# The second product of an MLP by Strassen's seven products, in one layer on one core

## The chip, the cores and the metric

The kernel runs on one core of a Trainium2 chip. The core has a matrix engine (TensorE, PE in the rows, with its weight loads as PEld), a vector engine (VectorE, DVE), an activation engine (ScalarE, ACT), a general engine (GpSimd, POOL) and SyncE (SP), which here only issues transfers. The metric is the device time of one execution in microseconds: 2275.08 us, the median of 3 runs (2274.39 to 2277.69).

## The reference, cut to what matters

One encoder layer in float32, with 512 tokens and a model width of 2048. Token mixing (two kinds of attention and an output projection), an MLP, and a gated injection follow each other, each between two norms. The change concerns the MLP alone:

```python
m = rms_norm(h, pre_mlp_norm[i]) @ w_up[i]            # 512 x 2048 by 2048 x 8192
m = jnp.square(jax.nn.relu(m)) @ w_down[i]            # 512 x 8192 by 8192 x 2048
h = h + rms_norm(m, post_mlp_norm[i])
```

The second line is the product in question: 512 tokens, a sum over 8192 hidden values, 2048 output columns.

## The kernel before, in words

Every product is computed to float32 accuracy from two halves: `split_out` (lines 191 to 193) writes a rounded high half `hi` on ScalarE (a copy to a type that TensorE takes) and the remainder `lo` on VectorE. A product of two such pairs is three matmuls, hi by hi, hi by lo and lo by hi (`mm3`, line 135). Weights arrive as tiles of 128 partitions by 1024 columns (512 KB), which hold two chunks of 128 rows by 512 output columns; `weights` (line 111) loads one into a buffer `raw` (3 of them) through SP's queue and splits it into two pairs `hi`, `lo` (4 buffers each).

The first product (lines 699 to 807) already runs by Strassen's seven products in Winograd's form: tokens, sum and output are cut into halves, sums of quarters are formed, and seven products take the place of eight. Its weight sums come about in two ways: an accumulating transfer that POOL issues (`accum_op`), or an addition on VectorE (lines 757 and 766). The squared hidden values go through the tensors `hdr` in HBM, which `h_out` (line 642) writes by transfers of 128 KB.

The second product (lines 810 to 852) is plain. It walks over eight blocks `fb` of eight chunks of the hidden values. For each block it loads the hidden values from `hdr` into `hring`, splits them into `hT`, and calls `tokmajor` (line 140): for each of four column pieces `n` of 512, four token tiles `i` of 128 accumulate in four PSUM banks over the block's eight chunks, then `d_done` adds them into `M` in SBUF on VectorE (line 839; a copy in the first block, line 837). The last block also takes the squares for the norm, multiplies by the gain `gpost` and starts the residual and the next norm (lines 840 to 846). The gains `gpost` and `gpre` are loaded at block 1, behind a part of `M` (`behind`, line 208, a tiny copy on POOL that makes a transfer wait).

The order of the instructions of each engine is laid out ahead of the run by a planner. It takes the program's order as the priority and a simulated time as the moment when each instruction could go, so an instruction may stand earlier or later than it is written. At run time each engine, and each transfer queue, takes its instructions in the planned order. On SBUF, tiles that carry one tag share memory: `O0`, `O1`, `X0` and `X1` are four large areas. In the first product `O0` holds the operands of products 5 and 6, `O1` those of 7 and 3, `X1` those of 1 and 2, `X0` the weight ring. A tile that takes over an area waits for the last reader of the one before. PSUM has eight banks: four with the tag `pj`, three `at`, one `o`.

## Time and profile before

| what | value |
|---|---|
| median of 3 runs | 2275.08 us |
| the profiled execution's own time | 2274.45 us |
| its span, first to last instruction | 2272.7 us |
| mean granted TensorE clock | 0.991 |
| TensorE busy | 2220.0 us (98%) |
| VectorE busy | 1375.5 us (61%) |
| ScalarE busy | 1091.3 us (48%) |
| first matmul of the second product | 1355.66 us |
| moved by transfers | 356.84 MB, 157 GB/s |

All rows below come from one profiled execution. Times within it count from its first instruction. Busy time is the time in which at least one instruction of the engine was running; matmuls overlap, so their count and their distance from each other say more than the duration of one. "Idle before" names the time an engine stood before the instructions of a group and what ended it. A granted clock of 1.00 is 2.4 GHz, 0.50 is 1.2 GHz.

### The profile page before, as it was taken

How to read it: one execution, taken by the hardware profiler on the slowest of the kernel's cores; microseconds unless marked ns; L12 is line 12 of the kernel's file. 1: busy time of each engine (PE TensorE's matmuls, PEld its weight loads, DVE VectorE, ACT ScalarE, POOL GpSimd, SP SyncE). 2: the span in 40 equal slices, each digit the busy share in tenths (PEclk: the TensorE clock that was granted, in tenths of full speed). 3: DMA queues.
4: the chain of work that ended last, by engine and by line, in shares of the span. 5: the costliest groups of instructions: out<-in, count | busy, mean ns of one | idle time of the engine just before them, and what ended most of it. 6: DMA issues, size and time to landing. Idle time of an engine off the chain costs nothing.

```text
span 2272.7 us, 30004 instructions
## 1 busy us (share of the span) xinstructions
PE 2220.0 (98%) x10899; PEld 1864.6 (82%) x10899; DVE 1375.5 (61%) x2248; ACT 1091.3 (48%) x2079; POOL 258.4 (11%) x385
## 2 busy tenths in 40 slices
PE   9999999999996799999999999999999999999997
PEld 7888888888785688888888888888888888888885
DVE  7567545555758677777777784443434434468446
ACT  5335433345656466666666673322323223257434
POOL 4320000000001121222122210000000000011002
PEclk9999999999998899999999999999999999999999
DMA  6222232236767988888887745434434433355435
GB/s 216 84 75 65 66 94 79 88 98 223 244 198 215 296 228 210 218 213 217 216 217 215 211 140 205 131 95 137 130 102 131 138 93 99 97 182 188 149 93 185
DMA packets 102084, 356.84 MB, mean 157 GB/s; under 512 B 13280, under 2 KB 14816, under 8 KB 101296
## 3 DMA queue, kind: packets, MB, share of 16 engines
q1 hardware_dynamic: 84432, 296.92, 41.1%
q0 software_dynamic: 17360, 58.01, 11.7%
q8 instruction: 85, 1.39, 0.3%
q14 instruction: 63, 0.52, 0.1%
q10 hardware_dynamic: 144, 0.01, 0.0%
HBM read 328.69 MB, written 26.18 MB: 156 GB/s over the span
## 4 chain that ended last, share of the span: by engine, by line
PE 91%; DVE 4%; ACT 1%; issue 1%; DMA 1%; POOL 1%; SPq 0%; DVEq 0%; ACTq 0%; POOLq 0%
PE tm L137 17%; PE tm L138 17%; PE tm L136 17%; PE ua L637 9%; PE ua L638 5%; PE ug L637 4%; PE ug L638 3%; PE qk L138 3%; PE qk L136 3%; PE qk L137 3%; PE ub L637 2%; PE ub L638 1%; PE ua L640 1%; DVE lo L131 1%; PE ug L640 1%
## 5 line engine op out<-in xcount | busy, mean ns | idle before, releaser
L130 ACT ACTIVATE hi<-raw 128x512 fp32r<-128x512 f32 x664 | 415.7, 631 | 806.6 <-PE tm L138 513.9
L131 DVE TENSOR_TENSOR lo<-raw,hi 128x512 fp32r<-128x512 f32 x664 | 454.1, 695 | 570.4 <-ACT hi L130 569.3
L137 PE MATMUL tm<-lo,hT 128*128 128x512 f32 x1024 | 398.6, 390 | 0.3 <-DVE lo L131 0.3
L138 PE MATMUL tm<-hi,hT 128*128 128x512 f32 x1024 | 398.3, 389 | 0.0
L136 PE MATMUL tm<-hi,hT 128*128 128x512 f32 x1024 | 370.8, 389 | 0.0
L637 PE MATMUL ua<-xc,uh 128*128 128x512 f32 x868 | 313.3, 396 | 15.8 <-ACT uh L192 15.8
L638 PE MATMUL ua<-xc,ul 128*128 128x256 f32 x992 | 259.1, 282 | 0.0
L137 PEld LDWEIGHTS tm<-lo,hT 128*128 128x128 f32 x1024 | 192.2, 188 | 40.6 <-DVE lo L131 0.7
L136 PEld LDWEIGHTS tm<-hi,hT 128*128 128x128 f32 x1024 | 192.2, 188 | 40.1 <-ACT hi L130 0.3
L138 PEld LDWEIGHTS tm<-hi,hT 128*128 128x128 f32 x1024 | 192.3, 188 | 39.8
L637 PEld LDWEIGHTS ua<-xc,uh 128*128 128x128 f32 x868 | 164.4, 189 | 49.5 <-ACT uh L192 16.6
L638 PEld LDWEIGHTS ua<-xc,ul 128*128 128x128 f32 x992 | 188.2, 190 | 13.6 <-DVE ul L193 0.9
L193 DVE TENSOR_TENSOR ul<-ring,uh 128x512 fp32r<-128x512 f32 x240 | 161.6, 689 | 55.7 <-PE ub L638 43.1
L637 PE MATMUL ug<-xc,uh 128*128 128x512 f32 x448 | 162.5, 397 | 10.4 <-ACT uh L192 10.4
L192 ACT ACTIVATE uh<-ring 128x512 fp32r<-128x512 f32 x240 | 148.6, 629 | 47.8 <-PE ub L640 25.2
L193 DVE TENSOR_TENSOR ul<-T,uh 128x512 fp32r<-128x512 f32 x192 | 130.1, 691 | 49.1 <-ACT uh L192 45.9
L192 ACT ACTIVATE uh<-T 128x512 fp32r<-128x512 f32 x192 | 117.3, 628 | 66.2 <-PE ua L637 39.3
L638 PE MATMUL ug<-xc,ul 128*128 128x256 f32 x512 | 133.9, 282 | 3.5 <-DVE ul L193 3.5
L137 PE MATMUL tm<-lo,xa 128*128 128x512 f32 x320 | 126.0, 394 | 4.5 <-DVE lo L131 4.5
L138 PE MATMUL tm<-hi,xa 128*128 128x512 f32 x320 | 125.4, 392 | 0.0
L136 PE MATMUL tm<-hi,xa 128*128 128x512 f32 x320 | 122.9, 394 | 1.0 <-ACT hi L130 0.6
L637 PEld LDWEIGHTS ug<-xc,uh 128*128 128x128 f32 x448 | 85.1, 190 | 27.1 <-ACT uh L192 10.7
(263 smaller groups left out, 3840.0 us busy)
## 6 DMA issues: line engine op xcount, KB each, us to landing
raw<-in_w_down SPq DMA_DIRECT2D x136, 512.0 KB, 3.6
ring<-in_w_up SPq DMA_DIRECT2D x128, 512.0 KB, 4.4
raw<-in_w_o SPq DMA_DIRECT2D x64, 512.0 KB, 4.0
raw<-in_w_gate SPq DMA_DIRECT2D x48, 512.0 KB, 4.2
raw<-in_w_in_t SPq DMA_DIRECT2D x39, 512.0 KB, 3.7
raw<-in_w_in_f SPq DMA_DIRECT2D x32, 512.0 KB, 3.6
hdr<-h POOLq DMA_DIRECT2D x128, 128.0 KB, 6.2
T<-in_w_up SPq DMA_DIRECT2D x32, 512.0 KB, 6.9
```

The lines of the kernel that those rows point to most:

```text
L130: nc.scalar.activation(hi, x, AF.Copy)
L131: nc.vector.tensor_sub(lo, x, hi.bitcast(F32))
L136: nc.tensor.matmul(o, lh, rh, start=start, stop=False)
L137: nc.tensor.matmul(o, lh, rl, start=False, stop=False)
L138: nc.tensor.matmul(o, ll, rh, start=False, stop=stop)
L192: nc.scalar.activation(hi, src, AF.Copy)
L193: nc.vector.tensor_sub(lo, src, hi.bitcast(F32))
L637: nc.tensor.matmul(o, hi[:, c], x, start=first and j == 0, stop=False, **on)
L638: nc.tensor.matmul(o[:, :256], lo[:, c], x[:, :256], start=False, stop=False, **on)
L640: nc.tensor.matmul(o, hi[:, c], x, start=False, stop=True, **on)
```

## The change

The second product is now computed by the same seven products. Tokens are cut into halves of 256 (`t`), output columns into halves of 1024 (`h`, each with two pieces `n` of 512), and the chunks of the sum into two halves by `half_of`: of each four chunks in a row, the first two belong to half 0 and the other two to half 1. A pair is one chunk of each half. There are 32 pairs. Blocks of 8, 8, 8 and 4 pairs go by seven products; the last four pairs (eight chunks) go through `tokmajor` as before, with the last block's `d_done`.

`hdr` is laid out by quarter, so that one transfer of 1 MB reads a quarter of a block's hidden values into `quad`. `op_work` forms the sums of quarters on VectorE and splits them into an operand `opt` (two operands share the tile `opt`). The products run in the order 1, 5, 6, 3, 7, 2, 4. The weight tiles stand in `xr` and `yr`, eight slots each: a slot's tile is loaded into `xr`, used by product 1, added to by an accumulating transfer of POOL, used by product 5, added to by VectorE (`sum_x`, after a lag of three slots), used by products 6 and 4; `yr` is loaded, added to by POOL after product 3, and loaded anew after product 7. `half_tiles` hands out buffers for the split halves of the weight tiles in turns of seven: four times a pair `hi` and `lo`, three times a `raw` buffer that holds both. A step of the loop over `todo` prepares the operand of the step two ahead (`AHEAD`), takes its share of `op_work` for the next product, and issues the twelve matmuls of its tile. Products 6, 7 and 4 accumulate onto the PSUM banks of product 1, product 3 onto those of product 5. After each product `add_out` takes each bank into `M` with a sign: on VectorE, or as a scaled copy on ScalarE for products 1, 5, 6 and 4 of the first block. The gains are loaded after the seven products.

```diff
-    hdr = [dram.tile([P, FB, S], F32, name=f"hdr{b}") for b in range(NFB)]
+    hdr = [dram.tile([P, 4, HB, 256], F32, name=f"hdr{b}") for b in range(FF // P // 2 // HB)]
+    def half_of(f):
+        return f // 2 % 2, 2 * (f // 4) + f % 2
...
-        nc.gpsimd.dma_start(hdr[f // FB][:, f % FB, t * 256:(t + 1) * 256], src)
+        odd, g = half_of(f)
+        nc.gpsimd.dma_start(hdr[g // HB][:, 2 * t + odd, g % HB, :], src)
...
     M = xo.tile([P, NT, D], F32, tag="O1", name="M")
+    NP2 = FF // P // 2
+    wdn = lambda n, odd, g: a["w_down"][n, g + odd]
+    blocks = [(g, min(HB, NP2 - CP - g)) for g in range(0, NP2 - CP, HB)]
+    ORDER = (1, 5, 6, 3, 7, 2, 4)
+    with phase("phdn") as pd:
+        quad = xo.tile([P, 4, HB, 256], F32, tag="O0", name="quad")
+        usum = pd.tile([P, HB, 256], F32, name="usum")
+        xr = xo.tile([P, 8, 1024], F32, tag="X0", name="xr")
+        yr = pd.tile([P, 8, 1024], F32, name="yr")
+        opt = xo.tile([P, 2, 2, HB, 256], F32R, tag="X1", name="opt")
...
+            n = halves[0]
+            halves[0] += 1
+            if n % 7 < 4:
+                return [wp.tile([P, 512], F32R, tag=t, name=f"d{t}{n}", bufs=NW) for t in ("hi", "lo")]
+            t = wp.tile([P, 2, 512], F32R, tag="raw", name=f"dhl{n}", bufs=NWRAW)
+            return [t[:, 0], t[:, 1]]
...
+                if p == 5:
+                    w.append(lambda Q=Q, U=U: V.tensor_sub(U, Q[A22], Q[A21]))
+                    w.append(lambda Q=Q: V.tensor_sub(Q[A21], Q[A11], Q[A21]))
+                elif p == 6:
+                    w.append(lambda Q=Q, U=U: V.scalar_tensor_tensor(Q[A11], U, -1.0, Q[A11], **minus))
+                elif p == 3:
+                    w.append(lambda Q=Q, U=U: V.scalar_tensor_tensor(U, Q[A12], -1.0, Q[A11], **minus))
+                w.append(lambda o=o, k=k, x=x: split_out(o[:, 0, k], o[:, 1, k], x))
...
+            if first and p in (1, 5, 6, 4):
+                nc.scalar.activation(m, o, AF.Copy, scale=float(sign))
+            elif sign > 0:
+                nc.vector.tensor_add(m, m, o)
+            else:
+                nc.vector.tensor_sub(m, m, o)
...
+            x = yr[:, slot] if p in (3, 7, 2) else xr[:, slot]
+            if p in (6, 4):
+                while late and (slot in late):
+                    sum_x(late.popleft())
+            w = parts2(x)
+            if p == 1:
+                nc.gpsimd.dma_start(x, wdn(n + 2, 0, g), accum_op=ALU.add)
+                nc.sync.dma_start(yr[:, slot], wdn(n + 2, 1, g))
+            elif p == 3:
+                nc.gpsimd.dma_start(x, wdn(n + 2, 0, g), accum_op=ALU.add)
+            elif p == 7:
+                nc.sync.dma_start(x, wdn(n, 1, g))
+            elif p == 4 and b + 1 < len(blocks):
+                g1, c1 = blocks[b + 1]
+                n1, kk = divmod(slot, c1 // 2)
+                if n1 < 2:
+                    x_load(n1, slot, g1 + 2 * kk)
+            if p in (5, 2):
+                late.append(slot)
+                if len(late) > LAG:
+                    sum_x(late.popleft())
...
+        for q in (A11, A22, A21, A12):
+            load_quad(0, q)
+            if q == A11:
+                for f in op_work(0, 0):
+                    f()
+                for n in range(2):
+                    for kk in range(4):
+                        x_load(n, n * 4 + kk, 2 * kk)
...
+                if b + 1 < len(blocks) and s >= 3:
+                    for q in {3: (A11,), 4: (A21,), 5: (A12,), 6: (A22,)}[s]:
+                        load_quad(b + 1, q)
+            if x + AHEAD < len(todo):
+                ready.append(operand(todo[x + AHEAD]))
+            left = c - slot
+            for _ in range(-(-len(work) // max(1, left - 2))):
+                if work:
+                    work.popleft()()
...
+            for j in range(2):
+                k = 2 * kk + j
+                hi, lo = w[j]
+                for i in range(2):
+                    t = slice(i * P, (i + 1) * P)
+                    sh, sl = op[:, 0, k, t], op[:, 1, k, t]
+                    o = acc[bank, i, n]
+                    nc.tensor.matmul(o, sh, hi, start=fresh and k == 0, stop=False, **on)
+                    nc.tensor.matmul(o, sh, lo, start=False, stop=False, **on)
+                    nc.tensor.matmul(o, sl, hi, start=False, stop=k == c - 1, **on)
...
-        GFB = 1
-        hring = xo.tile([P, 4, 2, S], F32, tag="X0", name="hring")
-        for fb in range(NFB):
...
+        gpost = bcast(pn, a["post_mlp"], D, "gpost2", M[:, 3, :])
+        gpre = bcast(pn, a["pre_ple"], D, "gpre2", M[:, 3, :])
...
+        tokmajor(lambda k, i: tuple(hT[:, q, hk[k], i * P:(i + 1) * P] for q in range(2)),
+                 wk("w_down"), ks, [(range(4), [0]), (range(4), [1]), ([0, 1], [2, 3]), ([2, 3], [2, 3])], d_done)
```

## Rows read from the trace of the kernel before

**Rows 1.** The page: busy time of three engines over the span, and TensorE and VectorE in 40 equal slices, in tenths.

```profile
PE 2220.0 (98%) x10899; PEld 1864.6 (82%) x10899; DVE 1375.5 (61%) x2248; ACT 1091.3 (48%) x2079; POOL 258.4 (11%) x385
...
PE   9999999999996799999999999999999999999997
...
DVE  7567545555758677777777784443434434468446
```

**Rows 2.** Windows of 100 us, one in the first product and two in the second: PE, PEld, DVE, ACT and POOL busy (instructions), then the granted clock, the share of the transfer engines and GB/s.

```profile
1000.00:1100.00 100.00, 100.00 (x575) 87.60 (x574) 77.57 (x120) 68.42 (x134) 21.85 (x33) 1.00 0.82 214
1400.00:1500.00 100.00, 100.00 (x443) 82.84 (x442) 41.43 (x63) 27.25 (x45) 0.00 (x0) 1.00 0.38 116
1900.00:2000.00 100.00, 100.00 (x443) 82.85 (x442) 39.50 (x59) 26.09 (x46) 0.00 (x0) 1.00 0.31 95
```

**Rows 3.** TensorE's waits in the whole run: what waited for what, us in total, times, the longest.

```profile
PE ua L637 <- ACT uh L192: 15.8, 2, 9.9
PE ug L637 <- ACT uh L192: 10.4, 1, 10.4
PE tm L137 <- DVE lo L131: 5.6, 6, 1.9
...
PE tm L136 <- ACT hi L130: 2.2, 4, 0.8
```

**Rows 4.** VectorE's timeline in the second product: start, us, instruction. The first additions into `M` of two column pieces in a row, and one in between.

```profile
1460.88 0.69 DVE L839 TENSOR_TENSOR M<-M,tm 128x512 f32<-128x512 f32 x1
1462.24 0.69 DVE L839 TENSOR_TENSOR M<-M,tm 128x512 f32<-128x512 f32 x1 [0.67 <-PE tm L138]
...
1482.64 0.69 DVE L839 TENSOR_TENSOR M<-M,tm 128x512 f32<-128x512 f32 x1
```

**Rows 5.** Timeline at the start of the first product: VectorE's 1024-wide and 512-wide operations back to back (merged, with their number at the end), and a 1024-wide copy on ScalarE.

```profile
734.18 3.50 DVE L193 TENSOR_TENSOR xc<-Af,xc 128x1024 fp32r<-128x1024 f32 x3
...
756.11 2.50 DVE L193 TENSOR_TENSOR ul<-ring,uh 128x512 fp32r<-128x512 f32 x4 [8.27 <-ACT uh L192]
...
734.31 1.06 ACT L192 ACTIVATE xc<-Af 128x1024 fp32r<-128x1024 f32 x1 [1.82 <-DVE Af L713]
```

**Rows 6.** Groups of instructions from 800 to 1300 us (first product): busy us, mean ns of one, idle time before them and what ended it.

```profile
L193 DVE TENSOR_TENSOR ul<-ring,uh 128x512 fp32r<-128x512 f32 x204 | 137.6, 689 | 40.1 <-PE ub L638 38.5 <-ACT uh L192 1.2
...
L192 ACT ACTIVATE uh<-ring 128x512 fp32r<-128x512 f32 x203 | 125.9, 629 | 38.6 <-PE ub L640 22.5 <-PE ug L637 10.2 <-PE ua L637 4.3
...
L757 DVE TENSOR_TENSOR T<-T,ring 128x1024 f32<-128x1024 f32 x26 | 31.9, 1225 | 0.9
...
L750 POOL DMA_DIRECT2D ring<-in_w_up x26 | 23.2, 891 | 248.8 <-DMA ring<-in_w_up 133.3 <-DVE h L658 68.1 <-DVE ul L193 27.1
```

**Rows 7.** Transfers. First the window of 10 us in which the transfer engines were full (columns as in rows 2), then, for 1000 to 1100 us, the two queues (packets, MB, share of 16 engines) and the issues with KB each and the median us to landing.

```profile
740.00:750.00 10.00, 4.70 (x16) 3.69 (x16) 3.75 (x4) 1.15 (x2) 0.87 (x1) 0.55 0.98 381
...
q1 hardware_dynamic: 3650, 13.26, 43.1%
q0 software_dynamic: 2434, 8.01, 38.0%
...
ring<-in_w_up POOLq DMA_DIRECT2D x6, 512.0 KB, 7.3
...
hdr<-h POOLq DMA_DIRECT2D x22, 128.0 KB, 6.6
T<-in_w_up POOLq DMA_DIRECT2D x5, 512.0 KB, 5.9
```

**Rows 8.** The handover between the two products: the copy behind the last group's product 6, SP's first transfer into the area of the weight ring, the last matmul of the first product and the first of the second.

```profile
1344.93 0.60 ACT L772 ACTIVATE kb<-ua 128x512 f32<-128x512 f32 x1 [1.11 <-PE ua L640]
...
1348.89 7.04 SPq L829 DMA_DIRECT2D hring<-hdr  x5
...
1355.43 0.40 PE L640 MATMUL ua<-xc,uh 128*128 128x512 f32 x1
1355.66 0.86 PE L136 MATMUL tm<-hi,hT 128*128 128x512 f32 x3
```

**Rows 9.** The start of the first product, where transfers crowd: a window (columns as in rows 2), a piece of the chain of waits (start, us, what), and TensorE's matmuls after a gap.

```profile
755.00:760.00 5.00, 3.87 (x12) 3.06 (x13) 2.66 (x5) 2.82 (x5) 0.00 (x0) 0.57 1.05 311
...
746.47 8.89 DMA ring<-in_w_up
...
756.13 0.79 PE L637 MATMUL ua<-xc,uh 128*128 128x512 f32 x1 [5.89 <-ACT uh L192]
...
758.51 0.63 PE L637 MATMUL ua<-xc,uh 128*128 128x512 f32 x1
...
759.15 0.47 PE L637 MATMUL ua<-xc,uh 128*128 128x512 f32 x1
```

**Rows 10.** The page: the weights of the plain products on ScalarE and VectorE (all of them, 512 wide), and transfers with KB each and the median us to landing.

```profile
L130 ACT ACTIVATE hi<-raw 128x512 fp32r<-128x512 f32 x664 | 415.7, 631 | 806.6 <-PE tm L138 513.9
L131 DVE TENSOR_TENSOR lo<-raw,hi 128x512 fp32r<-128x512 f32 x664 | 454.1, 695 | 570.4 <-ACT hi L130 569.3
...
raw<-in_w_down SPq DMA_DIRECT2D x136, 512.0 KB, 3.6
...
gpost<-in_post_mlp POOLq DMA_DIRECT2D x1, 1024.0 KB, 6.1
gpre<-in_pre_ple POOLq DMA_DIRECT2D x1, 1024.0 KB, 8.0
```

More of the change, by code (lines that the diff above doesn't have):

```diff
@@ L46 @@
 NWRAW, NW = 3, 4
-FB = 8
-NFB = FF // P // FB
+HB = 8
+CP = 4
 WARM = 11
@@ new lines, in layer, with d_done @@
+        gpost = bcast(pn, a["post_mlp"], D, "gpost2", M[:, 3, :])
+        gpre = bcast(pn, a["pre_ple"], D, "gpre2", M[:, 3, :])
+        for k in range(2):
+            pf = t512(f"pf{k}")
+            nc.sync.dma_start(pf, a["pT"][:, k, :])
+            split_out(pT[:, 0, k, :], pT[:, 1, k, :], pf)
+        def d_done(i, n, acc):
+            c = slice(n * 512, (n + 1) * 512)
+            m = M[:, i, c]
+            nc.vector.tensor_add(m, m, acc)
+            square_acc(ssq[i], n, m)
+            (nc.gpsimd if n == 2 else nc.vector).tensor_mul(m, m, gpost[:, c])
+            if n == 3:
+                if not Xg:
+                    Xg.append(new_x("xg"))
+                residual_norm(pn, M[:, i, :], ssq[i], i, hd[i], gpre, Xg[0], f"d{i}", r3[:, i:i + 1])
@@ L855, in layer @@
+        ks = range(FF // P - 2 * CP, FF // P)
+        hk = {k: half_of(k)[0] * CP + half_of(k)[1] - NP2 + CP for k in ks}
+        tokmajor(lambda k, i: tuple(hT[:, q, hk[k], i * P:(i + 1) * P] for q in range(2)),
+                 wk("w_down"), ks, [(range(4), [0]), (range(4), [1]), ([0, 1], [2, 3]), ([2, 3], [2, 3])], d_done)
         E = xo.tile([P, NT, D], F32, tag="O0", name="E")
```

117 lines of the change are left out of this document (84 added, 33 removed).

## The prediction

> **What bounds the kernel now.** I read the totals and the 40 slices first: TensorE is busy for 98% of the span and its digit is 9 in every slice but three, while VectorE has 61% and ScalarE 48% [rows 1]. The averages hide the stages, so the windows come next. In the stretch that the change rewrites (the second product, about 1356 to 2056 us) TensorE is busy all the time with 443 matmuls in 100 us at a granted clock of 1.00, VectorE for 40 of 100 us, ScalarE for 27, DMA for 38%; in the first product, which already runs by seven products, VectorE has 77.6 and DMA 82% and TensorE is still at 100 [rows 2]. The waits of TensorE confirm it: in the whole run it waited 5.6 and 2.2 us for weights of the plain products, and the large waits (15.8 and 10.4 us) are where the first product's stage begins [rows 3]. So the second product is bound by the number of its matmuls, and a matmul less is worth its full spacing. That spacing: the sums of one block of eight chunks into `M` begin 21.76 us apart, at 1460.88 and 1482.64 us, and between them lie 8 x 4 x 3 = 96 matmuls, so 0.2267 us each [rows 4]; the record of one shows 0.389 us because matmuls overlap.
>
> **What is removed.** Before, 64 chunks x 4 token tiles x 4 column pieces x 3 parts = 3072 matmuls. After, the blocks are 8, 8, 8 and 4 pairs of chunks (56 chunks) by seven products: 7 x 2 x c x 2 x 3 matmuls in a block of c pairs, with c summing to 28 that is 2352, against 2688 for the same chunks plain. The last eight chunks stay plain (384). 336 matmuls of the same shape go: 336 x 0.2267 = 76.2 us.
>
> The TensorE page of the Trainium skill ("TensorE: Matmul & The Clock Gate", section Back-to-back issue gap) gives about 131 ns for a sustained matmul of 512 columns in a stream with weight loads, and 216 ns for an isolated gap; no run here shows 131. By 131 the saving would be 44 us, by 216 it would be 72.6 us. The row of 0.2267 us decides, and nothing below uses the page's figures.
>
> **What is added on VectorE.** One step is one weight tile of 1024 columns: 12 matmuls, 2.72 us. A block of c = 8 has 56 steps, 152.3 us of TensorE. Back to back, a 512-wide operation starts every 0.60 us (four in 2.50) and a 1024-wide one every 1.14 us (three in 3.50) [rows 5]. In one block: 112 low halves x 0.60 = 67.5; 16 sums of weight quarters (`sum_x`) x 1.14 = 18.2; 14 low halves of the hidden values and 8 sums (`op_work`) x 1.14 = 25.0; 28 additions into `M` x 0.60 = 16.9. Together 127.6 us, 84% of the 152.3. In the first block 16 of the additions go to ScalarE, which leaves 118 us (77%, the load that the first product carries at full TensorE). The block of 4 has 28 steps, 76.2 us, and 33.8 + 9.1 + 12.5 + 16.9 = 72.3 us of VectorE, and 4.8 more for splitting the last plain chunks. By product the worst is product 6 of the short block: 12.9 us of work in 10.9 us (4.8 of splits, 1.1 of the next operand's split, 1.1 of a sum for it, 2.4 of additions, 3.4 of weight sums). Operands are prepared two steps (5.4 us) ahead, which takes up 2 us. I put 1 us on VectorE. The bounds: nothing, or, with whole durations instead of starts (0.69 and 1.22) and one idle 0.67 us before the second addition of each of the 14 pairs in a block (the wait of the additions in rows 4), 152 of 152.3 us in a long block (142.9 + 9.4) and 96 of 76.2 in the short one: 20 us. ScalarE has 112 x 0.63 and 14 x 1.06 = 85 us in 152 [rows 5, 6]; it hides, and the 16 copies add 10 us to the first block only.
>
> **What is added on DMA.** Each weight slot now takes three plain loads and two accumulating ones (before: four plain), and a block reads its hidden values in four transfers of 1 MB (two plain units of 512 KB each). A plain unit costs the engines 1.38 us when they are full (381 GB/s), 1.70 by share in the first product: 43.1 us for 13.26 MB [rows 7]. There the POOL queue took 38.0 us for 8.01 MB; with its 2.9 MB of stores at the plain rate (9.4 us) the 9.8 accumulating units are left with 2.9 us each, with the stores at nothing 3.9, and at twice the rate 1.9. Over a block (24 plain units for the eight slots, 8 for the hidden values, 16 accumulating) this is 32 x 1.38 + 16 x 2.9 = 91 us in 152: hidden on average. It is not even: the first product of a block asks for 8 accumulating and 8 plain units at once, 34 us in 21.8. The last of them is wanted 15 steps after the block begins, less a split of 1.3 us: 39.5 us. The stream begins two steps ahead less that split (4.1 us), and a landing takes some 4.4 us beyond the engines' time (7.3 less 2.9), so it lands at 34.2 + 4.4 - 4.1 = 34.5. Five us to spare: 0 in the second and third block. In the short block, 17.4 against 17.7: 0 as well.
>
> The first block is different, since nothing was loaded for it. Of what it needs, `quad` waits for the first product's sixth operand (its last reader ends at 1344.9 us), the weight ring `xr` for the ring before it (the first load into that memory went out at 1348.89) [rows 8]. The plan may send all four 1 MB transfers first, since they can go first: eight units of 1.38 = 11 us, and the first weight lands at 1345 + 11 + 1.4 = 1357.4, is split by 1358.7, against the first plain matmul at 1355.66 now [rows 8]: 3 us. It costs 0 if the weights go before the last three transfers, and 6 with the clock's part: after a gap of 5.9 us pairs of matmuls stood 0.64 us apart for 3.3 us, at a clock of 0.57, instead of 0.345, which loses 1.5 us [rows 9]. I take 3. Then the queue: 24 plain units and 8 accumulating ones are 33.1 + 23.4 = 56.5 us from 1345, with the landing 1405.9, wanted at 1358.7 + 39.5 = 1398.2: 7.7 us late; with an accumulating unit at 2.3 it is 2.9 late, at 1.9 in time, at 3.9 and plain at 1.70, 23 late. Rows 9 show that such a crowd holds TensorE up. I take 4, because in the full stretch a plain unit took 1.38 and not 1.70, and the accumulating ones should gain in the same way.
>
> POOL issues 16 accumulating transfers in a block at 0.89 us each [rows 6], 14 us of 152 with nothing else on its queue: nothing.
>
> **Where the plain chunks begin.** The last two steps hold their weights in the `raw` buffers (392 halves, seven to a turn; halves 389 to 391 are raw ones). The first plain weight can only be requested when half 389 is free, 2.7 us before the end of the seven products; landing 3.6, high half 0.63, low half 0.69 [rows 10]: 2.2 us late, of which the matmuls with the high half cover a little. I take 2; none if the plan finds another buffer, 5 if it asks at the end. What was done in the first block and now stands late (the two gains, `behind` a part of `M` that is written in the last product) has 21.8 us of plain matmuls before its first use, against 6.1 and 8.0 us to landing [rows 10]: nothing. The end of the kernel is as before.
>
> **Sum**, against the profiled execution's own 2274.45 us (span 2272.7 and 1.75 around it; 0.6 below the median of 2275.08): 2274.45 - 76.2 + 3 + 4 + 1 + 2 = 2208.3.
>
> **Rivals.** *The transfers do not keep up.* Plain units at 1.70 and accumulating ones at 3.9: the first block loses 23, the next two 5.6 each, the short one 5, with the other 6 the time is 2274.45 - 76.2 + 39 + 6 = 2243. For it: the first product's engines were at 82% with fewer plain bytes at a time. Against: full engines moved 381 GB/s. *VectorE's queue binds in part.* The 20 us above in place of 1, 2227; for it speaks 84% of the time in starts alone, against it that the waits before VectorE's halves in the first product came from TensorE still holding the buffers (38.5 us before `ul<-ring`), so it was ahead there [rows 6]. *Slower.* VectorE's queue is strictly in order. In the first product it idles 22.4 of 100 us, 0.62 us for each step of 2.78 [rows 2]. If these waits are not slack but handovers that stay with every step, a step costs 2.55 (whole durations, 142.9 us over 56 steps) + 0.62 = 3.17 us, 0.45 over TensorE's 2.72, over 196 steps 88 us, with the other 9: 2295. It decides at 0.39 us a step (76.2 / 196), a step of 3.11 us. Against it: the releasers just named. *Nothing is late*: 2198.
>
> **Numbers.** Forecast (2199 to 2222) 0.67; transfers 0.13; VectorE in part 0.10; slower 0.05; nothing late 0.05. Predicted 2208. The range runs from the bare sum less a run's spread, 2197, to the transfers' rival, 2243, and holds a little over 8 in 10. About 0.2% (4.5 us) is what a measurement can tell from none; only the slower rival and mixtures of stalls near 76 us lie there or beyond: faster 0.93, same 0.02, slower 0.05.
>
> **What would show it.** In the profile after: 2352 matmuls by seven products and 384 plain with 0.2267 us between them where nothing waits; TensorE waits of some us at the start of the stage, in the first two products of the first block, and before the first plain matmul, and near none in blocks two and three; VectorE at about 84% in these, 77% in the first; accumulating transfers landing within 10 us there. Wrong would be: TensorE waiting a little in each step with VectorE at 95% or more (its queue binds), or waiting once in each block in the fifth product for a weight that was added to (transfers), or matmuls farther apart without a wait.

## The result and the profile after

The changed kernel takes 2217.66 us (median of 4 runs, 2215.57 to 2218.66) against 2275.84 us for the kernel before in the same session: a ratio of 0.9743, with a 95% interval of 0.9726 to 0.976. The prediction was 2208, so the gain came, 58 us of it, and the losses beside it were about 10 us larger than the prediction put them.

The page of the kernel after, in the order of [rows 1] and with the slices of the granted clock:

```profile
PE 2152.6 (97%) x10563; PEld 1804.3 (81%) x10563; DVE 1571.1 (71%) x2477; ACT 1221.1 (55%) x2256; POOL 306.1 (14%) x441
...
PE   9999999999998599999999998999999999999997
...
DVE  7567645555667677777777777788789788677446
...
PEclk9999999999999699999999999999999999999999
```

TensorE is busy for 67.4 us less, with 336 records of matmuls fewer, and VectorE for 195.6 us more. In TensorE's line one new slice stands below 9, the 8 near 1360 us, where the new stage begins. TensorE's waits from there to the first plain chunks (columns as in [rows 3]):

```profile
PE da L993 <- ACT dhi L192: 4.4, 1, 4.4
PE da L994 <- DVE dlo L193: 3.7, 1, 3.7
PE tm L136 <- ACT hi L130: 2.0, 1, 2.0
PE db L994 <- DVE dlo L193: 0.4, 2, 0.3
```

Windows of the kernel after (columns as in [rows 2]): the start, three products of 22 us in the first block and in the second, two long stretches, and the handover to the plain chunks.

```profile
1350.00:1360.00 10.00, 5.63 (x31) 4.59 (x31) 9.50 (x12) 7.38 (x15) 1.62 (x3) 0.99 1.01 407
1360.00:1380.00 20.00, 16.35 (x59) 12.71 (x58) 16.61 (x23) 9.90 (x18) 6.61 (x8) 0.75 1.04 339
1380.00:1400.00 20.00, 20.00 (x90) 16.56 (x89) 16.23 (x21) 11.40 (x19) 0.86 (x1) 1.00 1.06 279
1454.00:1476.00 22.00, 22.00 (x97) 17.77 (x96) 18.61 (x25) 11.90 (x19) 0.00 (x0) 1.00 0.62 217
1476.00:1498.00 22.00, 21.73 (x95) 17.16 (x93) 20.04 (x27) 11.40 (x18) 0.00 (x0) 1.00 0.65 228
1498.00:1520.00 22.00, 21.92 (x97) 17.95 (x96) 20.62 (x30) 13.17 (x21) 1.73 (x2) 1.00 0.76 229
1520.00:1608.00 88.00, 88.00 (x390) 72.87 (x389) 68.99 (x95) 49.30 (x76) 12.08 (x14) 1.00 0.57 118
1608.00:1630.00 22.00, 21.79 (x95) 17.40 (x94) 18.14 (x24) 11.74 (x18) 0.00 (x0) 1.00 0.65 214
1630.00:1652.00 22.00, 21.76 (x95) 17.32 (x94) 20.11 (x27) 11.39 (x17) 0.00 (x0) 1.00 0.70 235
1652.00:1674.00 22.00, 21.91 (x97) 17.76 (x96) 21.70 (x32) 11.95 (x19) 1.39 (x2) 1.00 0.75 224
1674.00:1826.00 152.00, 152.00 (x672) 125.89 (x671) 126.42 (x175) 83.10 (x125) 13.51 (x17) 1.00 0.57 139
1900.00:1920.00 20.00, 17.96 (x73) 14.37 (x72) 8.61 (x14) 4.73 (x8) 1.43 (x4) 0.91 0.72 263
```

Read the number of matmuls, not the busy time: PE busy for 16.35 of 20 us holds 59 matmuls where a full stretch holds 90 in 20 us and 99 in 22 us (a matmul across an edge counts on both sides). So the losses can be placed, to about a matmul for each edge of a window. From the last matmul of the first product (1354.89 us) to the first plain one (1905.80) it is 550.9 us, and 2352 matmuls at 0.2267 are 533.2: the stage loses 17.7 us. **Start**: the first matmul is 4.5 us late and 31 are missing from 1360 to 1380, 11.6 us in all. **Middle**: 18 matmuls are missing in the two groups of three windows; timed from matmul to matmul it is 3.8 us, 1.7 in the first block and 2.1 in the second, and nothing in the third. **Before the plain chunks**: a wait of 2.0 us. The plain stretch itself takes 92.7 us against 91.0 for the last 384 matmuls before, the tail behind it 218.2 against 216.4, the stage began 0.5 us earlier, and before the change the same chunks lost 0.4: -76.2 + 17.7 + 1.7 + 1.8 - 0.5 - 0.4 = -55.9, by which the two profiled executions differ (2218.55 and 2274.45).

What stood ahead of the first splits, on VectorE's timeline (start, us, instruction):

```profile
1355.33 2.36 DVE L869 TENSOR_TENSOR usum<-quad 128x1024 f32<-128x1024 f32 x2 [0.47 <-PE ua L644]
...
1360.21 1.22 DVE L870 TENSOR_TENSOR quad<-quad 128x1024 f32<-128x1024 f32 x1
1361.34 1.22 DVE L193 TENSOR_TENSOR opt<-usum,opt 128x1024 fp32r<-128x1024 f32 x1
1362.48 1.22 DVE L872 SCALAR_TENSOR_TENSOR quad<-usum,quad 128x1024 f32<-128x1024 f32 x1
1363.61 1.89 DVE L193 TENSOR_TENSOR dlo<-xr,dhi 128x512 fp32r<-128x512 f32 x3
```

VectorE made the operands of products 5 and 6 (`op_work`) from 1355.33 to 1363.6 us and only then the first low half of a weight, for which TensorE was standing. The tile itself had landed at 1358.52, and ScalarE, which had its share of the same operands first, wrote the high half from 1358.99.

### The profile page after: what moved, and what is told of

Same layout as the page of the kernel before. It is cut to its first block, busy times and chain, and to the rows that moved or that the text cites. A ratio compares the mean times of both kernels' runs of the same rounds, so it can differ in the third digit from the quotient of the medians.

```text
span 2216.7 us, 29930 instructions
## 1 busy us (share of the span) xinstructions
PE 2152.6 (97%) x10563; PEld 1804.3 (81%) x10563; DVE 1571.1 (71%) x2477; ACT 1221.1 (55%) x2256; POOL 306.1 (14%) x441
## 4 chain that ended last, share of the span: by engine, by line
PE 85%; DVE 8%; DMA 4%; ACT 2%; issue 2%; POOL 0%; SPq 0%; DVEq 0%; ACTq 0%; POOLq 0%
PE ua L641 9%; PE tm L137 8%; PE tm L138 8%; PE tm L136 8%; PE ua L642 5%; PE ug L641 5%; PE da L994 4%; PE da L995 4%; PE da L993 4%; PE ug L642 3%; PE qk L138 3%; PE qk L136 3%; PE qk L137 3%; PE ub L641 2%; PE dg L994 2%; PE dg L995 2%
## 5 line engine op out<-in xcount | busy, mean ns | idle before, releaser
L131 DVE TENSOR_TENSOR lo<-raw,hi 128x512 fp32r<-128x512 f32 x440 | 305.7, 704 | 285.6 <-ACT hi L130 284.8
L130 ACT ACTIVATE hi<-raw 128x512 fp32r<-128x512 f32 x440 | 274.3, 631 | 387.9 <-PE tm L138 166.3
L192 ACT ACTIVATE dhi<-xr 128x512 fp32r<-128x512 f32 x127 | 79.0, 629 | 67.1 <-PE da L995 25.2
L641 PEld LDWEIGHTS ug<-xc,uh 128*128 128x128 f32 x448 | 85.1, 190 | 26.7 <-ACT uh L192 10.2
L642 PEld LDWEIGHTS ug<-xc,ul 128*128 128x128 f32 x512 | 97.4, 190 | 9.3 <-DVE ul L193 4.8
L994 PE MATMUL da<-dlo,opt 128*128 128x512 f32 x252 | 99.8, 396 | 3.9 <-DVE dlo L193 3.7
L137 PE MATMUL tm<-lo,xg 128*128 128x512 f32 x256 | 99.9, 390 | 1.0 <-DVE lo L131 0.8
L136 PE MATMUL qk<-xa,hi 128*128 128x512 f32 x256 | 100.6, 393 | 0.0
L137 PE MATMUL tm<-lo,O 128*128 128x512 f32 x256 | 100.4, 392 | 0.0
```

The source lines that it names most:

```text
L130: nc.scalar.activation(hi, x, AF.Copy)
L131: nc.vector.tensor_sub(lo, x, hi.bitcast(F32))
L136: nc.tensor.matmul(o, lh, rh, start=start, stop=False)
L137: nc.tensor.matmul(o, lh, rl, start=False, stop=False)
L192: nc.scalar.activation(hi, src, AF.Copy)
L641: nc.tensor.matmul(o, hi[:, c], x, start=first and j == 0, stop=False, **on)
```

## The experiments

All twelve were timed beside the kernel before; e5, e6 and e8, whose work or blocks differ, are told in their own places. The losses of each row come from one profiled execution. "Start" is what the first 385 matmuls of the stage lost (to about 1440 us), "middle" what the next lost to the end of the second block, both timed from matmul to matmul against 0.2267 us each; the stage's loss is reckoned as above (where the start was reordered, in e2, e7, e9, e10 and e12, two of its matmuls ran ahead of the last of the first product, and the stage's loss is 0.5 us too small). The first product's end differs by up to 5.5 us between profiles of the same code, so a few us are read from the stage and not from a median.

| run | median us | ratio to before (95%) | stage loses | start | middle | before plain |
|---|---|---|---|---|---|---|
| after | 2217.66 | 0.9743 (0.9726-0.976) | 17.7 | 11.6 | 3.8 | 2.0 |
| e1_order | 2217.07 | 0.9739 (0.9724-0.9753) | 16.3 | 10.0 | 3.5 | |
| e2_x_first | 2231.16 | 0.9802 (0.9787-0.9817) | 32.5 | 26.0 | 4.5 | |
| e3_turn | 2216.78 | 0.9735 (0.9719-0.9751) | 12.6 | 10.4 | 2.9 | 0 |
| e4_no_sum | 2221.73 (1 run) | | 16.8 | 11.5 | 0 | 5.0 |
| e7_start | 2218.94 | 0.9745 (0.9731-0.976) | 17.6 | 12.4 | 3.8 | |
| e9_yr_late | 2216.03 | 0.9732 (0.9719-0.9745) | 17.8 | 13.1 | 2.7 | 1.8 |
| e10_both | 2216.9 | 0.9732 (0.9717-0.9747) | 15.5 | 14.1 | 2.5 | 0 |
| e11_plain_acc | 2212.96 (1 run) | | 12.6 | 10.4 | 0 | 1.9 |
| e12_all | 2210.76 | 0.9711 (0.9698-0.9724) | 8.9 | 5.8 | 1.1 | 0 |

**e1_order: VectorE's order at the start.**

```
with tc.issue_after(high and low half of the tile two steps ahead):   # first block, s < 2
    work.popleft()()
```

> The first block lost 11.4 us at its start (9 us of waiting less two matmuls, then some 6 us at half clock). Theory A, order: VectorE and ScalarE were planned to make the operand of product 5 (eight operations of 1024, 1355.3 to 1363.6 us) before the first weights' halves. Here that work is held behind the halves of the first three weight tiles on both queues, and nothing else is changed; the transfers go in the same order. A expects the first matmul near 1358 us and no second wait for a low half, a start loss of about 4 us, and a time 6 to 8 us under the changed kernel (2210). Theory B, transfers: the first weight lands late behind the four transfers of 1 MB, so the order of the queues matters little. B expects the first matmul not before 1359.6, its low half as late as before, and 2216 to 2218.

The median did not move: the time is theory B's. The first matmul came 4.0 us late in place of 4.5 and the second wait, 3.7 us, was gone, as theory A had it, but products 5 and 6 lost 2.7 us, which they had not before, and product 1 still lost 3.4. Two windows and one piece of the chain of waits (start, us, what), in order of time:

```profile
1373.04 20.45 DMA xr<-in_w_down
...
1380.00:1400.00 20.00, 17.72 (x76) 13.73 (x74) 15.72 (x20) 13.59 (x23) 0.00 (x0) 1.00 1.01 291
1400.00:1420.00 20.00, 19.73 (x84) 15.73 (x85) 20.00 (x28) 11.21 (x18) 0.00 (x0) 1.00 0.16 54
```

A transfer that adds to a weight tile took 20.45 us to land, with the engines full. So VectorE's order was a loss, and behind it stood the transfers.

**e2_x_first: the weights ahead of three `quad` transfers.**

```
for q in (A11, A22, A21, A12):
    if q != A11:
        behind(quad[:, q, 0], xr[:, {A22: 1, A21: 3, A12: 5}[q]])
    load_quad(0, q)
```

> Three of the four transfers of 1 MB are held (by a tiny copy on POOL) until weight slots 1, 3 and 5 have landed; no order on VectorE or ScalarE is imposed. The first weight should land near 1353 us. A and B both expect the first matmul at about 1355.5 us and a start loss of 0 to 1 us, unless the operand work of product 5 is still ahead of the halves. What the prediction put at 4 us (the weights that are added to land late for product 5 of the first block) should show now if it was only covered by the late start: by the prediction's price a wait of 3 to 8 us in product 5, time 2210 to 2214; if that price was too high, no wait there, time 2206 to 2208.

The first matmul came without a wait, and against both expectations the kernel lost 13.5 us more than the changed one: VectorE stood 8.2 us for A22 and 8.7 for A12. A12 stood in SP's queue behind the loads of `yr`. In no trace here has SP more than eight transfers on the way; with eight out, A12 was issued at 1372.42, when the first `yr` load had landed (1372.34). From the chain of waits, and a window:

```profile
1356.00 16.34 DMA yr<-in_w_down
1372.42 28.02 DMA quad<-hdr
...
1380.00:1400.00 20.00, 6.54 (x14) 4.13 (x14) 11.86 (x12) 8.70 (x14) 0.00 (x0) 0.63 1.04 306
```

**e7_start and e9_yr_late: everything in the order in which it is wanted.** e7 has SP's queue as A11, two weight tiles, A22, one, A21, five, A12, the edit of e1, and each `yr` load of the first block three steps later. e9 moves these to where product 5 reads the tile it adds to (and lets the sums of that product stand five steps behind in place of three):

```
if b == 0 and p == 5:
    behind(yr[:, slot], xr[:, slot])          # a copy of one column on GpSimd
    nc.sync.dma_start(yr[:, slot], wdn(slot // 4 + 2, 1, 2 * (slot % 4)))
```

> The start of the stage put in the order in which its pieces are wanted: A11, then the first two weight tiles ahead of A22, one more ahead of A21, the other five, and A12 last; the plain loads of the second rows (yr) of the first block three steps later each, behind a landed tile; product 5's and 6's operands made on VectorE and ScalarE only behind the splits of the weight tile two steps ahead. Same work, same bytes. Theory (the 11 us at the start are a crowd of transfers in the wrong order plus VectorE's order, and the bytes as a whole fit): first matmul of the stage at or before the end of the first product plus 1 us, no wait over 2 us in product 5, the stage loses 17.5 - 10 = about 7 us in place of 17.5, and the kernel takes about 2208. Rival (the first 40 us are bound by their bytes in total, 24 plain units and 8 accumulating ones, so what is saved at the start comes back in product 5, as in the run with VectorE's order alone): waits of 8 us or more at accumulated weights or at A22 and A21 in product 5, and 2216 to 2219.

> As the run with the start put in order, but each plain load of second rows (yr) of the first block now waits until the accumulated tile of the same slot has landed, so that in product 1 and 5 only what these want is under way: after 1348.3 us 8 units for the weight tiles, 4 for A22 and A21 and 8 accumulating ones, 12 x 1.38 + 8 x 2.9 = 40 us, in place of 54. Same work and bytes in all. Theory (the start is a matter of order: what is wanted in the first 40 us fits into them): no wait over 2 us in products 1 and 5, the stage loses about 8 us in place of 17.5, and the kernel takes 2207 to 2210; the yr tiles are then wanted in product 6 (from 1391 us, 2.7 us apart) and land 8 to 12 us after their issue, which may cost 1 or 2 us there. Rival (bytes in total: what is moved out of one product is missing in the next): 8 us or more of waits in products 5 and 6, and 2215 to 2219.

Both missed, and the times are those of the rivals: 12.4 and 13.1 us at the start. In e9 product 5 was nearly full (85 of 90 matmuls from 1380 to 1400 us), and the loss had moved into products 1 (6.2 us) and 6 (6.1). GpSimd's and VectorE's timelines of e9 show why in product 6:

```profile
1393.59 18.72 POOL L212 COPY yr<-xr 128x1 f32<-128x1 f32 x1 [3.34 <-DMA xr<-in_w_down]
...
1410.96 1.30 DVE L195 TENSOR_TENSOR dlo<-xr,dhi 128x512 fp32r<-128x512 f32 x2
1415.89 1.23 DVE L902 TENSOR_TENSOR xr<-xr,yr 128x1024 f32<-128x1024 f32 x1 [3.62 <-DMA yr<-in_w_down]
```

The copy of a single column, the last of eight, ends at 1412.31 us, right behind the VectorE instruction that ends at 1412.26 and is followed by VectorE's first pause since the copy began. Until then the last `yr` load could not be issued.

**e11_plain_acc: what the accumulation costs the transfer engines.**

```
-nc.gpsimd.dma_start(x, wdn(n + 2, 0, g), accum_op=ALU.add)
+nc.gpsimd.dma_start(x, wdn(n + 2, 0, g))
```

> The changed kernel with its accumulating transfers made plain ones of the same size from the same queue at the same places (the weights are then not added up, which leaves out that part of the computation); nothing else differs. Theory (an accumulating unit takes the engines 2.9 us against 1.38, and this is what keeps them full until 1401.7 us): the transfers' share falls from above 1 at about 1344 + 32 x 1.38 = 1388 to 1390 us, with 380 GB/s or more all the way, and landings of these tiles in the first block fall from 15.2 to 10 us or less. The start's losses were put down to VectorE's order and to quad going first, not to the accumulating ones, so the kernel takes 2214 to 2218 all the same. Rival (the crowd is one of queues and issues, not of the accumulation): full until about 1400 as now, near 280 GB/s.

As the first theory had it. The queues from 1370 to 1390 us, where the engines are full (q0 is GpSimd's, q1 SP's; packets, MB, share of 16 engines), first of the kernel after, then of e11:

```profile
q0 software_dynamic: 750, 2.74, 68.7%
q1 hardware_dynamic: 749, 2.73, 36.4%
```

```profile
q0 software_dynamic: 1138, 4.14, 52.1%
q1 hardware_dynamic: 1219, 3.96, 49.9%
```

A unit of 512 KB (0.524 MB) that is added took 0.687 x 20 / (2.74 / 0.524) = 2.63 us of the engines, a plain one 1.40; in e11 the same queue needed 1.32 for it. The crowd ended at about 1390 us in place of 1401.7, and the added tiles of the first block landed in 10.2 us (median) in place of 15.2. The start lost about as much as before (10.4 us). The kernel was faster than expected (one run) by the middle, where nothing was lost any more.

**e3_turn: which buffer is free for the first plain weight.**

```
-if n % 7 < 4:
+if (n + 4) % 7 < 4:
```

> The turn of seven is shifted by four, so that the last two steps keep their halves in the buffers hi and lo, and the raw buffers are free three steps before the end of the seven products. Theory C: the 2.0 us wait and the half clock behind it (3.9 us together) before the first plain matmul come from the raw buffer that is asked for late; expects no wait there and a time 3 to 4 us lower (2214). Rival: the wait moves to the buffers hi and lo, under 1 us gained (2217).

```profile
1900.00:1920.00 20.00, 20.00 (x90) 16.56 (x89) 12.56 (x21) 5.07 (x8) 2.97 (x4) 1.00 0.71 260
```

The wait and the half clock behind it are gone (17.96 us, 73 matmuls and 0.91 before the edit), the stage loses 5.1 us less, of which 2.0 lie at the start and in the middle, where the edit does nothing. From the beginning of the last block to the last plain matmul 3.9 us were gained, as much as theory C names. The median shows 0.9 us, which lies within the spread.

**e4_no_sum: VectorE without the sums of weights.** `sum_x` is left out.

> Leaves out the additions of yr to xr on VectorE (16 in a block of eight, so products 6 and 4 use other weights than they should). In the changed kernel TensorE issued 8 and 10 matmuls fewer than at full pace around product 2 of the first and second block (1.8 and 2.3 us). Theory D: VectorE's load there is the cause (20 of 22 us busy); expects full pace, 99 matmuls in each 22 us, and about 4 us less (2213 to 2214). Rival E: VectorE stands for the next block's quarter of hidden values (1.96 us at 1490 us), which stays; expects the same loss within 1 us.

The middle ran full (99, 99, 99, 99, 98 and 98 matmuls in the six windows); the time of its one run did not fall, with 5.0 us of waiting before the plain chunks in place of 2.0 and a first product that ended 2.5 us later. I first read this as VectorE's load; e11, which leaves that load as it is, runs full too, so it cannot be the load alone. VectorE's waits in the kernel after name the other reason:

```profile
DVE xr L900 <- DMA yr<-in_w_down: 15.9, 7, 4.7
```

The longest stands at 1451.8 to 1456.2 us. The sum that product 4 wants may be made as soon as product 7's reload of `yr` has landed, and it was placed early in VectorE's queue, ahead of low halves that product 7 was waiting for. Such a wait does not always cost. In e11 it reads

```profile
DVE xr L900 <- DMA yr<-in_w_down: 9.2, 7, 3.1
```

and nothing was lost. Together with the waits for the next block's quarter of hidden values (the rival E), VectorE stood 7.6 and 8.0 us in blocks one and two of the kernel after, and 1.7 and 2.1 us were lost; 5.6 and 4.3 us in e11 and 3.4 us in block three of the kernel after (waits over 0.4 us each) cost nothing. So VectorE seems to have some 4 to 6 us to spare in a block, and what it stands beyond that comes out on TensorE. No run changed the waits alone.

**e5_no_third and e6_pool_sum: how much VectorE has left.**

```
-nc.tensor.matmul(o, sl, hi, start=False, stop=k == c - 1, **on)        # e5
-nc.vector.tensor_add(xr[:, slot], xr[:, slot], yr[:, slot])            # e6
+nc.gpsimd.tensor_add(xr[:, slot], xr[:, slot], yr[:, slot])
```

> Leaves out the third part (low half of the hidden values times high half of the weights) of every matmul of the seven products: 784 matmuls fewer, so the output is not the reference's; all transfers, splits, sums and additions stay. TensorE then wants 101.5 us in a long block in place of 152.3, and what VectorE or the transfers need by themselves comes to light. Theory A (VectorE's need is the sum of its starts, as the prediction had it: 118 us in the first block, 127.6 in the second and third, 72 in the short one): the stage of the seven products takes about 455 us (551 now), the kernel about 2124, VectorE is busy 95% or more in blocks 2 and 3 and TensorE's waits are at VectorE's halves. Theory B (VectorE needs whole durations and handovers, 152 us a long block, which is why 4 us are lost in the middle already): the stage takes some 530 us and the kernel about 2200. Theory C (transfers bind before VectorE): TensorE's waits are at weight tiles that landed late, with DMA at 95% or more outside the first block.

> The sums of weight quarters (sum_x, 56 of them) are made on GpSimd in place of VectorE, which takes 18 us of 152 from VectorE in a long block. If the 4 us lost around products 7 and 2 in the second and third block come from VectorE's load, the windows there go back to 89 or 90 matmuls in 20 us, and the kernel to about 2213.5. If the additions on GpSimd (whose duration no row of this kernel shows for 1024 columns) hold up the accumulating transfers that are issued from the same queue, waits for weights that were added to appear in products 5 and 7, and the time stays at 2218 or rises, by 10 us or more where a sum takes longer than a step of 2.7 us.

e5 took 2146.44 us (one run) and its stage 477 us, nearer to theory A (2124 and 455) than to B (2200 and 530). The first additions of product 2 in three blocks, on its VectorE timeline, with VectorE busy for 97% of the time between them:

```profile
1474.80 1.27 DVE L887 TENSOR_TENSOR M<-M,db 128x512 f32<-128x512 f32 x2
...
1604.23 1.27 DVE L887 TENSOR_TENSOR M<-M,db 128x512 f32<-128x512 f32 x2
...
1737.36 1.28 DVE L887 TENSOR_TENSOR M<-M,db 128x512 f32<-128x512 f32 x2
```

With TensorE's need down to 101.5 us a block takes 129.4 and 133.1 us, near the 127.6 of the starts alone and far from 152. VectorE is no bound of the changed kernel; on the average it leaves some 20 us in each long block. e6 took 2248.73 us, ratio 0.9882 (0.9866 to 0.9899), 31 us slower than the changed kernel. A group of GpSimd and one of VectorE in it:

```profile
L900 POOL TENSOR_TENSOR xr<-xr,yr 128x1024 f32<-128x1024 f32 x52 | 142.2, 2741 | 74.3 <-DMA yr<-in_w_down 38.3 <-DVE dlo L193 24.8 <-DVE dhl L193 11.0
```

```profile
L193 DVE TENSOR_TENSOR dlo<-yr,dhi 128x512 fp32r<-128x512 f32 x17 | 19.6, 1173 | 4.2 <-ACT dhi L192 4.1
```

The sum takes 2.74 us on GpSimd against 1.22 on VectorE, and VectorE's low halves beside it take 1.17 in the mean of this group and 0.84 to 0.96 in the three others, against 0.69. GpSimd's additions hold VectorE up, and TensorE's waits in the stage, but for 4.4 us at the start, are at VectorE's low halves (23.7 us). The expectation had looked for waits at the accumulating transfers.

**e8_cp2: two plain pairs in place of four.**

```
-CP = 4
+CP = 2
```

> Two pairs of chunks left plain in place of four: the last block of the seven products has 6 pairs, 24 matmuls fewer in all (7 x 2 x 2 x 2 x 3 = 168 more by seven products, 192 fewer plain), 5.4 us by 0.2267 us. If nothing else changes, 2212.3. Where it would go the other way: the plain stretch is 43.5 us in place of 92.7, and the gains and the transfers of the last stage that it covered may come late, which would show as waits after the last plain matmul (the tail was 218.2 us); VectorE in a block of 6 is loaded as in the long ones, so the last block may lose 1 to 2 us as the second and third do.

2219.09 us, ratio 0.9743 (0.9726 to 0.9759): no gain. The 24 matmuls went, 5.4 us, and most of it was lost again: the wait before the first plain weight grew from 2.0 to 3.5, the third block lost 1.8 us in place of nothing, and a wait of 0.9 us for a low half stands right behind the last plain matmul. (That one came 4.0 us earlier, at 1994.5 us, and the tail is 221.5 us in place of 218.2, but 16 matmuls, 3.6 us, which ran among the plain ones before now run behind them.)

**e10_both and e12_all: together.** e10 is e9 with the turn of e3. e12 makes three more edits: the small copy on ScalarE, right behind the split of the same tile, the sums behind the newest low half, and each split of a weight behind the one before, so that the halves keep their order on both engines.

```
with tc.issue_after(the same tile's high half):
    nc.scalar.activation(yr[:, slot, :1], xr[:, slot, :1], AF.Copy)
...
with tc.issue_after(newest low half):
    nc.vector.tensor_add(xr[:, slot], xr[:, slot], yr[:, slot])
...
with tc.issue_after(both halves of the split before):
    split_out(hi, lo, x[:, j * 512:(j + 1) * 512])
```

> The start as in the run before it, and the turn of the half buffers shifted by four, so that the first plain weight finds a free buffer: no wait before the first plain matmul, 4 to 5 us less at that place (the run with the turn alone showed 20.00 of 20 us there). If the two places are independent: 2203 to 2206. If the start's gain does not come: 2211 to 2214.

> All of it together, three places that can be read apart. Start: the order of the run before with yr late, but the small copy that holds each yr load back is on ScalarE, right behind the split of the same tile, in place of GpSimd, whose last copy there stood from 1393.6 to 1412.3 us, until VectorE paused. Middle: the sums of weight quarters (sum_x) are held behind the low half of the newest split on VectorE, so that in product 7 none stands in VectorE's queue for a yr load that has not landed (15.9 us of waits in the second part of the stage now, 4.75 the longest); the low halves keep their order. End: the turn of the half buffers shifted by four. Theory for the middle (it was VectorE standing for a transfer, not VectorE's load): 89 or 90 matmuls in every 20 us from 1454 to 1680, with VectorE's busy time unchanged; rival (its load): 95 to 97 matmuls in 22 us there as now. Theory for the start (GpSimd's copy made the second half of the loss): the loss to 1440 us falls from about 12 to 6 us; rival (bytes in total): it stays at 11 to 12. With all three right the kernel takes 2203 to 2206, with the end alone 2213.

e10 kept the gain at the end and lost again at the start (67 matmuls of 90 from 1400 to 1420 us). e12 is the fastest, 0.9711 of the kernel before with all five runs (2209.80 to 2213.24) below those of the changed kernel, but 5 to 8 us above its expectation. Its windows:

```profile
1360.00:1380.00 20.00, 17.66 (x69) 11.80 (x67) 10.46 (x13) 7.78 (x15) 5.54 (x8) 1.00 1.05 293
1380.00:1400.00 20.00, 19.52 (x85) 15.72 (x85) 20.00 (x26) 15.21 (x34) 0.86 (x1) 1.00 1.04 316
1400.00:1420.00 20.00, 20.00 (x90) 16.57 (x89) 18.36 (x25) 10.70 (x19) 0.00 (x0) 1.00 0.23 95
...
1454.00:1476.00 22.00, 22.00 (x98) 18.22 (x98) 16.13 (x24) 12.02 (x18) 0.00 (x0) 1.00 0.56 207
1476.00:1498.00 22.00, 22.00 (x98) 18.22 (x98) 22.00 (x28) 11.92 (x18) 0.00 (x0) 1.00 0.58 196
1498.00:1520.00 22.00, 21.69 (x95) 17.34 (x95) 19.64 (x27) 12.74 (x22) 2.58 (x3) 1.00 0.76 225
...
1608.00:1630.00 22.00, 22.00 (x99) 18.22 (x98) 16.76 (x24) 12.02 (x19) 0.00 (x0) 1.00 0.48 176
1630.00:1652.00 22.00, 22.00 (x98) 18.22 (x98) 22.00 (x28) 11.28 (x17) 0.00 (x0) 1.00 0.59 189
...
1880.00:1900.00 20.00, 18.28 (x76) 13.58 (x75) 19.05 (x30) 8.19 (x15) 2.18 (x4) 1.00 0.41 131
1900.00:1920.00 20.00, 20.00 (x90) 16.57 (x89) 8.08 (x13) 5.88 (x11) 0.00 (x0) 1.00 0.52 184
```

The start loses 5.8 us, where the theory said 6: product 6 (from 1405 us) is full now that GpSimd is out of it. The clock stays at 1.00. What is left lies in product 1 and the beginning of product 5, with the engines above 1.0; that it is the bytes themselves was not tried by moving fewer. The landings speak for the order: from the fourth on, product 1's weights landed 3.0 to 3.8 us apart (1364.27 to 1378.69), more than its step of 2.72 us, while GpSimd's added tiles for product 5 went through the engines beside them; the first of those landed at 1365.90, and product 5 began at 1382.6. An estimate from the units above: A11, A22, A21, eight weights and eight added tiles, 14 x 1.40 + 8 x 2.63 = 40.6 us from 1345, would be through by 1386, before product 5 wants its last tile (about 1400). An order that serves product 1 first was not tried.

In the middle no sum waits for a transfer any more, and the loss is 1.1 us, where it was 3.8 in the kernel after and 2.5 to 4.5 in the six other runs that left the middle alone; VectorE's busy time is not less. So most of that loss was not the load, but whether it was the wait or the order of the halves this run does not part. What is left stands at the end of product 4, where ScalarE now waits for sums (3.1 us in the first block). The 14 matmuls missing from 1880 to 1900 us are new, and come from the same edit: in the short block ScalarE waited 9.3 us for two sums that were held back.

## Why the prediction came out as it did

**The matmuls: right.** 336 went, and where nothing waits 90 of them run in 20 us, as in [rows 2] (443 in 100) and [rows 4]. The term of 76.2 us needed no correction.

**The first weight: 3 us predicted, 11.6 measured.** The step that failed is "is split by 1358.7". The landing was 1.1 us off (1358.52, predicted 1357.4 with all four `quad` transfers ahead of it). But the low half was ready at 1364.3, 5.6 us later than that step had it, behind 8 us of operand work for products 5 and 6, which the plan put first as it could go first; and in the window from 1360 to 1370 us, after the two gaps, the granted clock stood at 0.50, as it had stood at 0.57 in [rows 9]. The 11.6 us are 4.5 to the first matmul, 3.7 for its low half and 3.4 at the lower clock, which the forecast had not taken into its 3. (The upper bound of 6 for this place does not follow from its own 3 and 1.5.) I had listed the operand work in the sum for VectorE and not asked where in its queue it would stand.

**The first block's transfers: 4 us predicted, none in their place.** The size of a unit was nearly right: 2.63 and 1.40 us measured, 2.9 and 1.38 from [rows 7]. The engines were full until 1401.7 us, by the forecast's sum until 1401.5 (1345 + 56.5), and the last added tile landed at 1400.5, where 1405.9 was reckoned. No wait showed in product 5 because it began at 1388.5, 8 us later than the forecast had it, and its need had moved by as much. The two terms hang together: e1, e2, e7 and e9 each shortened one and got the other, and e12 still pays 5.8 us. Their sum, 7, was too small for the kernel as it was built.

**VectorE: 1 us predicted, 3.8 measured, by another way.** The sum over starts held: 126.42 of 152 us busy from 1674 to 1826 (83%, predicted 84%), and e5 measured the floor. So the rival in which the handovers stay with each step (2295) and the one by whole durations (2227) were wrong in their mechanism. The loss came with a queue in order that stood for transfers, which the argument had looked for on TensorE only; that the waits are its cause is read from traces side by side and from e12, not shown by them alone.

**The first plain weight: 2 us predicted, 2.0 waited,** and by the reason given, as e3 shows; the clock of 0.91 in the window behind it was left out; it costs about what the plain stretch is longer, 1.7 us. Of the 1.8 us in the tail, 1.1 is a longer wait for one weight of the last product (1.6 us against 0.5); what in the change causes it stays open.

**The rival in which the transfers do not keep up** (2243) lay on the right resource and had the wrong extent: blocks two and three had no wait for a weight that was added to, and there these landed in 5.3 to 10.2 us. Its accumulating unit of 3.9 us was 1.3 too long.

The total came out near the forecast because the term of 76.2 us is so much larger than the losses: the four small terms were put at 10 us together and came, with the tail, to about 20 in the profile.

## What to carry to other kernels

When a stage begins cold, write down for each engine's queue what stands in it ahead of the first operand, not only when that operand lands; work that can go early will. A sum that waits for a transfer belongs behind the work that the next step needs, since a queue in order passes its wait on to everything after it, but not so far behind that its own reader waits, as in e12's last block. And where reordering moves a loss about, look at the resource that all orders share, here the transfer engines in the first 45 us, and at what goes through it ahead of its need.

## What the runs showed of the hardware

An accumulating transfer cost the engines 1.9 times a plain one of the same size (2.63 against 1.40 us for 512 KB), and e11 shows that this lies in the accumulation and not in the queue.

SP has at most eight transfers on the way in every trace of this case. In the kernel after it issued the first loads of `yr` at 1358.60, 1359.93 and 1361.50 us, when the tiles of `xr` issued eight places before them had landed (1358.52, 1359.91 and 1361.49).

A copy of one column on GpSimd stood for 18.72 us in e9 while VectorE ran 22 instructions with two operands back to back, and ended 0.05 us after VectorE's first pause; in e10 the same copy stood for 17.73 us and ended 0.03 us after the first pause. The seven copies before it, in both, took some 5 us together while VectorE was as busy, so it is not so each time. With 1024-wide additions on GpSimd (2.74 us each, 1.22 on VectorE) VectorE's low halves of weights took 0.84 to 1.17 us in the mean of four groups in place of 0.69, while its additions into `M`, which read one operand from PSUM, kept 0.68. GpSimd's issues of accumulating transfers kept their 0.86 us.

The Trainium skill ("SBUF — State Buffer", section "SBUF: two separate sides") says that the two engines share a pair of ports by an exclusive lock, held for a whole instruction, also by a VectorE instruction with two inputs in SBUF, against a GpSimd instruction that reads SBUF. The rows of e6, e9 and e10 agree with such a lock; that GpSimd can stay locked out over a whole row of VectorE's instructions is what the 18.72 and 17.73 us add.
